# Projections of x in pairs by seven products over half of K, values loaded for two heads, keys doubled on GpSimd

## The chip, the cores and the metric

The kernel is one program on one core of a Trainium2 chip. The core has TensorE (PE; its weight loads are listed apart as PEld), VectorE (DVE), ScalarE (ACT), GpSimd (POOL) and SyncE (SP), which issues nearly all DMAs. The metric is the device time of one execution in microseconds. Before the change it is 2416.11 us, the median of three runs (2416.07 to 2419.38).

## The reference

The model is an encoder of two layers over 1024 tokens of width 1024, in float32. In each layer x is normalised and projected once; the columns of the projection belong to four groups of attention heads, which run side by side; their outputs are normalised, joined and projected back, and an MLP with squared ReLU follows.

```python
h = rms_norm(x, norm1_g[l])
proj = h @ w_in[l]
(a_cq, a_ckv, a_kr, b_q, b_k, b_v, c_q, c_k, c_v, d_q, d_k, d_v) = jnp.split(proj, splits, axis=-1)
y_a = mla_mixer(a_cq, a_ckv, a_kr, ...)      # A: latent attention, dense, 4 heads
y_b = diff_mixer(b_q, b_k, b_v, ...)         # B: difference of two softmaxes, dense, 4 heads
y_c = swa_mixer(c_q, c_k, c_v, sinks[l], ...)  # C: window of 128, 4 query and 2 key heads
y_d = na_mixer(d_q, d_k, d_v, na_rpb[l])     # D: neighbourhoods on a 2-D grid, 4 heads
mix = jnp.concatenate([rms_norm(y_a, ...), y_b, rms_norm(y_c, ...), rms_norm(y_d, ...)], axis=-1)
x = x + mix @ w_out[l]
h = rms_norm(x, norm2_g[l])
x = x + jnp.square(jax.nn.relu(h @ w_up[l])) @ w_down[l]
```

In front of A's attention stands a second projection: `a_cq` and `a_ckv` (the latents) are normalised by their own rows and multiplied by small matrices.

## The kernel before

**Numbers.** x lies transposed on the chip, as eight tiles of 128 features by 1024 tokens. Float32 matmuls go in three passes (`passes`): a weight is split into a high part `wh` and a low part `wl`, an operand into `xh` and `xl`, and wh·xh, wh·xl and wl·xh are added up in a bank of PSUM. A split (`split`) is one ACT instruction that writes the high part and one subtraction that writes the low one, on DVE for x and on GpSimd for the weights of the projections.

**Projections.** The columns of `w_in` are laid out as 15 tiles of 128 (`T_BQ`, `T_DK` and so on; A's are `T_CQ`, `T_CQR`, `T_CKV`) and the values of B and D apart in `w_v`. Three tiles go in an opening wave while x is being split (`several`), the values in `values`, and the other twelve by `one`: per tile the weights are loaded and split, and for each half of 512 tokens eight tiles of K in three passes make 24 matmuls of 128x512 in one bank. Then `ev` evicts the bank on DVE: times the row norms `rb`, for B and C with the rotary tables `tabc` and `tabs`, and the result is split again (tile `both`) and stored to HBM, from where the attention loads it in its own layout. `proj_latent` does A's tiles; it sums the squares of the latents (tiles `lsq`) by small matmuls on PE, makes the reciprocal roots on ACT and DVE, stores them as rows in HBM (`drows`) and loads them spread. `latent_up` then multiplies the latents (`latp`) by the second matrices.

**Attention.** Scores are matmuls of tiles `stack` (queries and keys with their high and low parts on top of each other, so that for D and C the key's 64 rows stand twice in a tile of 128), softmax is on DVE and ACT (tile `p`), PE transposes the probabilities (`ident,p`) and multiplies them by the values (`pt,v`). A's scores end in matmuls on tiles `corner`. `mix` are the attention's outputs as operands of the output projection, which is followed by the MLP (`far`, `opa`, `opb`, `opc`). The MLP is already built of seven products on halves of the tokens, of K and of the columns.

**Order.** No loop sets the order on the engines. Every instruction is first recorded (`Plan.add`), with what it reads and writes; `Plan.order` then walks through a model of the five queues and takes, on each engine, the ready instruction of lowest rank. Ranks come from a table `SPAN` by stage ('open', 'b1', 'lat', 'pd', 'pc', 'up', 'b', 'd', ...), limits on buffers from `ROOM` and `CAPS`. So projections, attention and the latents' second step are interleaved on PE, and each engine gets one fixed list. All are emitted from one line, L717, so the profile's rows are told apart by the names of tiles.

Of the kernel before, what the change touches and what calls it, by code (L numbers as in the profile page):

```python
# [23 lines left out]
P = 128  # L24
# [248 lines left out]
class Plan:  # L273
# [106 lines left out]
    def price(self, s):  # L380
# [3 lines left out]
        if op == "dma_start":  # L384
# [19 lines left out]
            per = (run / 20.7 if run >= 512 else 19.6 + run / 28.3) * (1.3 if few else 1.0)  # L404
# [190 lines left out]
    def issue(self, s, t):  # L595
# [13 lines left out]
        if q == "tensor":  # L609
# [13 lines left out]
            s.done = t + max(occ * (2 if s.tiled else 1), 220) + 180 * (1.5 if slow else 1)  # L623
# [10 lines left out]
class Place:  # L634


    def __init__(self, plan, bufs=1):
# [5 lines left out]
    ROOM = {'a4.0': 36, 'a4.1': 31, 'act10.0': 63, 'act10.1': 56, 'b4.0': 6, 'b4.1': 7, 'bias3.0': 4,  # L643
# [33 lines left out]
class Trunk:  # L677
# [106 lines left out]
    def product(self, ps, ws, xs, n, start=True, stop=True):  # L784

        last = len(ws) - 1
        for k, (w, x) in enumerate(zip(ws, xs)):
            self.passes(ps, w, x, slice(n * 512, n * 512 + 512), start and k == 0, stop and k == last)
# [1401 lines left out]
```

## Time and profile before

The profiled execution took 2422.19 us in all, its span is 2420.4 us; the three timed runs have a median of 2416.11 us.

| | busy us | share of the span | instructions |
|---|---|---|---|
| PE | 2387.2 | 99% | 12060 |
| DVE | 1861.2 | 77% | 3490 |
| ACT | 1300.1 | 54% | 2406 |
| POOL | 378.1 | 16% | 273 |

The mean granted clock of PE is 0.997, and 387.21 MB are moved by DMA, 160 GB/s on the average. A row of a group of instructions reads: line, engine, operation, what it writes and reads, shapes, how many; then busy us, mean ns of one; then the engine's idle time just before them and what ended it. The matmul's mean is from its start to a modelled end and overlaps the next one; the pace is the time of a stretch over its matmuls. A plain float32 matmul (`pt,v`, and the small ones on columns of ones) stands twice in the trace's counts.

### The profile page before, as it was taken

The numbers are of one execution on the slowest core, as the hardware profiler recorded it, in microseconds if no ns is written. First come the engines' busy times: TensorE is split into PE (matmuls) and PEld (weight loads), VectorE is DVE, ScalarE is ACT, GpSimd is POOL, SyncE is SP. The second block draws the span as 40 slices with busy tenths as digits, with TensorE's granted clock in tenths as the row PEclk, the third lists the DMA queues.
The fourth block names the chain that finished last, engine by engine and source line by source line (L and its number), as shares of the span: only waits on it lengthen the run. The fifth ranks groups of instructions, "written<-read, shape, count | busy, mean of one in ns | idle before, by whom it ended". The sixth has DMA issues, their size and how long they took to land.

```text
span 2420.4 us, 34855 instructions
## 1 busy us (share of the span) xinstructions
PE 2387.2 (99%) x12060; PEld 1904.4 (79%) x12060; DVE 1861.2 (77%) x3490; ACT 1300.1 (54%) x2406; POOL 378.1 (16%) x273
## 2 busy tenths in 40 slices
PE   9999999999999999999999999999999999999998
PEld 7877766778788888888887777767788888888887
DVE  6687776777977779778858778767598777898778
ACT  5555676664644445344435667676564444544446
POOL 4253025023000000000033231430410000000000
PEclk9999999999999999999999999999999999999999
DMA  6444798731444466443454376894514444755442
GB/s 204 135 139 136 190 256 240 181 123 55 140 147 158 160 219 203 151 150 109 153 166 113 114 188 178 240 253 125 170 46 161 152 147 158 243 166 166 137 136 92
DMA packets 213953, 387.21 MB, mean 160 GB/s; under 512 B 41720, under 2 KB 60304, under 8 KB 213776
## 3 DMA queue, kind: packets, MB, share of 16 engines
q1 hardware_dynamic: 198800, 358.76, 49.5%
q10 hardware_dynamic: 14976, 26.22, 2.9%
q8 instruction: 95, 1.56, 0.3%
q14 instruction: 82, 0.67, 0.1%
HBM read 268.80 MB, written 116.09 MB: 159 GB/s over the span
## 4 chain that ended last, share of the span: by engine, by line
PE 73%; DVE 6%; DMA 3%; ACT 2%; issue 1%; POOL 1%; SPq 0%; DVEq 0%; POOLq 0%; ACTq 0%
PE bank L717 73%; DVE p L717 1%; DVE x L717 1%; DVE part L717 1%; DMA ws<-in_w_out 1%; DMA rz<-drows 1%; DVE ev L717 1%; SPq L717 0%; DMA tabc<-in_c 0%; ACT p L717 0%; DVE far L717 0%; DMA drows<-row 0%; DVE xl L717 0%; DVE wl L717 0%; DVE sq L717 0%
## 5 line engine op out<-in xcount | busy, mean ns | idle before, releaser
L717 PE MATMUL bank<-far,wh 128*128 128x512 f32 (+1 forms) x2848 | 869.0, 387 | 0.0
L717 PEld LDWEIGHTS bank<-far,wh 128*128 128x128 f32 x2848 | 532.1, 188 | 109.5 <-ACT wh L717 0.9
L717 PE MATMUL bank<-far,wl 128*128 128x512 f32 (+1 forms) x1424 | 550.1, 387 | 1.8 <-DVE wl L717 1.7
L717 ACT ACTIVATE p<-p,col 128x1024 f32<-128x1024 f32 (+2 forms) x320 | 294.0, 920 | 97.4 <-DVE col L717 93.2
L717 POOL TENSOR_TENSOR wl<-ws,wh 128x512 fp32r<-128x512 f32 (+1 forms) x122 | 162.7, 1340 | 1016.3 <-DVE x L717 598.7
L717 PEld LDWEIGHTS bank<-far,wl 128*128 128x128 f32 x1424 | 267.5, 188 | 57.9 <-DVE wl L717 3.6
L717 DVE TENSOR_TENSOR x<-bank,x 128x512 f32<-128x512 f32 (+1 forms) x276 | 187.4, 682 | 125.7 <-PE bank L717 125.1
L717 PE MATMUL bank<-stack 96*128 96x512 f32 (+3 forms) x768 | 237.7, 391 | 2.0 <-DMA va<-part 0.9
L717 PE MATMUL bank<-ident,p 128*128 128x128 f32 x1376 | 219.6, 275 | 5.2 <-DVE p L717 4.5
L717 PEld LDWEIGHTS bank<-ident,p 128*128 128x128 f32 x1376 | 164.5, 140 | 44.2 <-issue 10.3
L717 PE MATMUL bank<-xh,wh 128*128 128x512 f32 x480 | 189.3, 405 | 1.6 <-ACT xh L717 1.5
L717 PE MATMUL bank<-xl,wh 128*128 128x512 f32 x480 | 190.2, 407 | 0.4 <-DVE xl L717 0.4
L717 DVE CUSTOM_DVE_ANT_0 p<-bank,zero 128x512 f32<-128x512 f32 x192 | 129.4, 686 | 79.0 <-PE bank L717 77.2
L717 PE MATMUL bank<-xh,wl 128*128 128x512 f32 x480 | 189.6, 406 | 0.4 <-POOL wl L717 0.4
L717 ACT ACTIVATE pt<-bank 128x512 f32<-128x512 f32 (+2 forms) x256 | 137.3, 558 | 92.9 <-PE bank L717 80.3
L717 ACT ACTIVATE far<-act 128x512 fp32r<-128x512 f32 x224 | 134.6, 622 | 86.8 <-DMA act<-acts 83.8
L717 DVE TENSOR_TENSOR wl<-raw,wh 128x512 fp32r<-128x512 f32 x224 | 153.6, 690 | 27.2 <-ACT wh L717 26.6
L717 PE MATMUL bank<-pt,v 128*64 128x256 f32 (+2 forms) x1344 | 164.4, 389 | 1.3 <-ACT pt L717 0.8
L717 PE MATMUL bank<-mix,wh 128*128 128x512 f32 x512 | 160.8, 394 | 3.5 <-ACT mix L717 2.6
L717 PEld LDWEIGHTS bank<-stack 128*128 128x128 f32 (+1 forms) x768 | 135.4, 189 | 35.2 <-issue 9.0
L717 ACT ACTIVATE ev<-ev 128x512 f32<-128x512 f32 x128 | 80.8, 632 | 139.5 <-DVE ev L717 136.5
L717 DVE CUSTOM_DVE_ANT_0 p<-bank,zero,col 128x512 f32<-128x512 f32 x192 | 142.4, 747 | 14.1 <-PE bank L717 5.6
(188 smaller groups left out, 3958.6 us busy)
## 6 DMA issues: line engine op xcount, KB each, us to landing
act<-acts SPq DMA_DIRECT2D x224, 256.0 KB
raw<-in_w_up SPq DMA_DIRECT2D x128, 256.0 KB
acts<-ev SPq DMA_DIRECT2D x128, 256.0 KB
acts<-ev ACTq DMA_DIRECT2D x96, 256.0 KB
c<-in_w_down SPq DMA_DIRECT2D x64, 256.0 KB
ws<-in_w_in SPq DMA_DIRECT2D x60, 256.0 KB
rz<-drows SPq DMA_DIRECT2D x40, 256.0 KB
ws<-in_w_out SPq DMA_DIRECT2D x40, 256.0 KB
```

The lines of the kernel that those rows point to most:

```text
L717: getattr(s.eng.engine, s.op)(*[real(a) for a in s.args], **{k: real(a) for k, a in s.kw.items()})
```

## The change

Each of the twelve tiles now goes together with another one: (BQ1, BK1), (CQ, CKV), (DK1, CQR), the two of DQ, the two of C's queries, (CK, CV). Of the eight tiles of K, two of the first four and their partners four further (`DEEP` = 2: tiles 0, 1 and 4, 5) are treated as a 2 x 2 block product: the two halves of tokens, the two halves of K and the two tiles of columns make seven products of blocks in place of eight. The other four tiles of K are multiplied as before. The products share banks of PSUM: a bank is read in between (by ACT into a tile `sum`, or by a DVE sum), and more products are accumulated into it.

For that, `sums` makes, once a layer, four combined operands for each of two tiles of x and their partners (tiles `tx`), overwriting the two tiles of x in place, and `two` makes combined weights from the loaded tiles `wr` on GpSimd, in pieces of two tiles of K (256 columns). The evictions read `sum` for part of the tiles. x's parts are now kept by halves of tokens. The stages b1, lat, pd, pc become 'vals', 'sums' and 'px', in which the latents come second, ahead of D's and C's tiles.

The loads of values take two heads at once (`vpair`: runs of 128 numbers in HBM, where they were 64), in B and D. The keys of D and C are loaded once into the first 64 partitions of their tile, and `again` copies them to the other 64 on GpSimd. `SPAN`, `ROOM` and two of the planner's costs (of DMAs, and of the end of a matmul) have new numbers.

```diff
-        def one(t, xs, ev):
-            ws = self.wtile(w_in(t))
-            for n in range(2):
-                ps = self.mm_ps()
-                self.product(ps, ws, xs, n)
-                ev(n, ps)
-                yield True
+        def two(ts, evs):
+            raw = []
+            for t in ts:
+                for c, w in enumerate(self.twin("wr", bufs=3)):
+                    raw.append(w.rearrange("p (k c) -> p k c", k=4))
+                    self.load(raw[-1], w_in(t)[c])
+            a, b, c, e = raw
+            J = self.DEEP
+            near = lambda t: t[:, :J]
+            add = partial(self.tt, eng=nc.gpsimd)
+            plain = [[xs[k + h][n] for h in (0, 4) for k in range(J, 4)] for n in range(2)]
+            def parts(*srcs):
+                wh, wl = (self.wp.tile([P, 4, P], R, tag="wd" + p, bufs=4, name="w" + p) for p in "hl")
...
+                    self.split(wh[:, sl], wl[:, sl], t, eng=nc.gpsimd)
...
+            def copy(ps):
+                t = self.place.tile([P, 512], F, tag="sum", bufs=3, name="sum")
+                nc.scalar.activation(t, ps, AF.Copy)
+                return t
+            def join(t, ps):
+                self.tt(t, ps, t, ALU.add)
+            u, q, r = self.bank("u"), self.bank("q"), self.bank("q")
+            wa = parts(a)
+            self.block(u, wa[:J], ops[1])
+            c11 = copy(u)
+            wb = parts(b)
+            self.block(q, wb[:J], ops[2])
+            self.block(q, wa[J:] + wb[J:], plain[0], False)
+            join(c11, q)
+            evs[0](0, c11)
+            self.block(r, wa[J:] + wb[J:], plain[1])
+            s1 = near(self.half_weights())
+            add(s1, near(c), near(e), ALU.add)
+            add(near(c), near(a), near(c), ALU.subtract)
+            add(near(a), s1, near(a), ALU.subtract)
+            add(near(b), near(b), near(a), ALU.subtract)
+            yield True
+            p = self.bank("p")
+            w5 = parts(s1, c[:, J:])
+            self.block(p, w5[:J], ops[5])
+            c12 = copy(p)
+            w6 = parts(near(a), near(c))
+            self.block(u, w6[:J], ops[6], False)
+            join(c12, u)
+            self.block(r, parts(near(b)), ops[3], False)
+            join(c12, r)
+            evs[0](1, c12)
+            yield True
+            self.block(u, w6[J:], ops[7], False)
+            c22 = copy(u)
+            we = parts(e)
+            self.block(p, w5[J:] + we[J:], plain[1], False)
+            join(c22, p)
+            evs[1](1, c22)
+            self.block(u, we[:J], ops[4], False)
+            self.block(u, w5[J:] + we[J:], plain[0], False)
+            evs[1](0, u)
+            yield True
+        def sums():
...
+            ops.update({1: [xs[k][0] for k in J], 2: [xs[k + 4][0] for k in J],
+                        3: [xs[k + 4][1] for k in J], 4: [], 5: [], 6: [], 7: []})
+            def parts(i, src):
+                t = self.place.tile([P, 2, 512], R, tag="tx", bufs=8, name="tx")
+                ops[i].append(self.rows_split((t[:, 0], t[:, 1]), src))
+            for k in J:
...
+                self.tt(t, v, t, ALU.subtract)
+                nc.scalar.activation(t, t, AF.Copy, scale=gk)
+                parts(5, t)
+                less(t, hi, t)
+                parts(6, t)
+                nc.scalar.activation(v, v, AF.Copy, scale=gk)
+                less(v, hi, v)
+                parts(7, v)
+                less(t, lo, t)
+                parts(4, t)
...
-        with at("b1"):
-            run_all(one(T_BQ[1], xs, self.ev_rope(tabs, qb[:, 1])))
-            run_all(one(T_BK[1], xs, self.ev_rope(tabs, kb[:, 1])))
+        with at("vals"):
             values(r)
+        with at("sums"):
+            sums()
...
+        with at("px"):
+            run_all(two((T_BQ[1], T_BK[1]), [self.ev_rope(tabs, qb[:, 1]), self.ev_rope(tabs, kb[:, 1])]))
+            run_all(self.proj_latent(l, two, d_keys(1), rb, tabs, lat, krd, rows))
             run_all(proj_d())
-        with at("pc"):
             run_all(proj_c())
...
-    BANKS = {"mm": 8, "tr": 4, "sb": 2, "pv": 2}
-    EARLY, NP = 4, 6
+    BANKS = {"mm": 8, "tr": 4, "sb": 2, "pv": 2, "u": 1, "p": 1, "q": 2}
+    EARLY, NP, DEEP = 4, 6, 2
...
+    def vpair(self, src, t):
+        v = self.place.tile([P, 8, P], F, tag="vv", bufs=2, name="vv")
+        self.load(v, src[:, :, t * P:t * P + P].rearrange("t p d -> p t d"))
+        return [v[:, :, j * 64:j * 64 + 64] for j in range(2)]
+    def again(self, k):
+        self.nc.gpsimd.tensor_copy(k[64:128], k[0:64])
...
-                    self.load(k[0].bitcast(F)[half], kd[0, t, rows])
-                for i in range(2):
-                    self.load(k[1].bitcast(F)[i * 64:i * 64 + 64], kd[1, t, rows])
+                    self.load(k[i].bitcast(F)[0:64], kd[i, t, rows])
+                for s in k:
+                    self.again(s)
```

The order of the instructions shows this at two places. Over the whole list PE has 11270 matmuls and transposes before and 11198 now.

The first place is on PE in layer 0, where the sums of the latents' squares are made (`lsq`; `stack` are scores, 384 columns wide for D and C and 512 for B, `ident,p` transposes, `x` and `wh` a projection). Before:

```order
L717 MATMUL bank_102<-pt,v 64x256 x16
L717 MATMUL bank_106<-stack 128x256 x2
L717 MATMUL bank_105<-stack 128x256 x2
L717 MATMUL bank_101<-lsq,square 32x256 x4
L717 MATMUL bank_101<-lsq,pairs 16x256 x4
L717 MATMUL bank_101<-lsq,more 32x256 x4
L717 MATMUL bank_103<-stack 128x384 x2
L717 MATMUL bank_100<-stack 128x384 x2
L717 MATMUL bank_107<-ident,p 128x128 x3
L717 MATMUL bank_104<-ident,p 128x128
L717 MATMUL bank_106<-ident,p 128x128
L717 MATMUL bank_104<-ident,p 128x128
```

Now:

```order
L717 MATMUL bank_107<-ident,p 128x128 x2
L717 MATMUL bank_100<-pt,vv 64x256 x16
L717 MATMUL bank_106<-lsq,square 32x256 x4
L717 MATMUL bank_106<-lsq,pairs 16x256 x4
L717 MATMUL bank_106<-lsq,more 32x256 x4
L717 MATMUL bank_101<-ident,col_72 8x128
L717 MATMUL bank_105<-stack 128x512
L717 MATMUL bank_102<-stack 128x512
L717 MATMUL bank_104<-stack 128x512
L717 MATMUL bank_103<-x_249,wh 128x512 x2
L717 MATMUL bank_107<-stack 128x512
L717 MATMUL bank_100<-x_354,wh 128x512
```

Before, all projections lie ahead of these rows, scores of D or C stand around them, and the first `latp` stands 118 rows later. Now a pair of D's tiles begins behind them, scores of B stand around them, and the first `latp` stands 455 rows later. Ahead of the first corner of A then lie, counted from the first `latp`, 109 transposes of probabilities in layer 0 (before: 66) and 112 in layer 1 (before: 128).

The second place is on POOL, at the end of layer 0's projections: `wl<-wr,wh` are low parts of weights, `part<-part` and `both<-part,both` C's rotary sums and low parts, `y<-y,rz` an output times its denominators. Before, no copies stand there. Now:

```order
L717 TENSOR_TENSOR wl<-wr,wh 128x256 x3
L717 TENSOR_TENSOR wl<-wr,wh 128x512
L717 COPY stack<-stack 64x1024 x2
L717 TENSOR_TENSOR part<-part 128x4x8x8 x2
L717 TENSOR_TENSOR both<-part,both 128x512 x2
L717 COPY stack<-stack 64x1024 x6
L717 TENSOR_TENSOR wl<-ws,wh 128x512
L717 COPY stack<-stack 64x1024 x4
L717 TENSOR_TENSOR y<-y,rz 128x1024
```

The twelve copies of a layer come behind the last low parts of the projections' weights; two of them stand ahead of the last rotary sums of C, and A's first low part (`wl<-ws,wh`) stands behind eight. On SP the loads `stack<-kd` and `stack<-kc` of a layer fall from 24 to 12 and those of B's and D's values from 8 to 4.

More of the change, by code (lines that the diff above doesn't have):

```diff
@@ L991, in d_keys @@
+        ops = {}
         def d_keys(t):
@@ L994, in proj_d @@
         def proj_d():
-            for t in range(2):
-                yield from one(T_DQ[t], xs, self.ev_plain(rb, self.to_parts(qd[:, t], 0.125)))
-            yield from one(T_DK[1], xs, d_keys(1))
+            yield from two(T_DQ, [self.ev_plain(rb, self.to_parts(qd[:, t], 0.125)) for t in range(2)])
         def values(r):
@@ L1199, in ev @@
             c, s = tabs
-            if rows and n == 0:
+            done = len(ys)
+            if rows and not ys:
                 ys.extend([self.part(), self.part()])
@@ L1288, in ev @@
             self.latent_parts(y, self.gq[:, l, 1:2], 64, n, lat[:, 1], squares[1])
-        yield from one(T_CQR, xs, ev)
+        yield from two((T_DK[1], T_CQR), [keys, ev])
         with self.plan.sooner(15):
@@ L1717, in attn_c @@
             for n, k in enumerate(ks[kv]):
-                for i in range(2):
-                    self.load(k.bitcast(F)[i * 64:i * 64 + 64], run(kc[n, kv]))
+                self.load(k.bitcast(F)[0:64], run(kc[n, kv]))
+                self.again(k)
         for g in range(2):
```

80 lines of the change are left out of this document (46 added, 34 removed), and 58 rows, old and new, of tables (ROOM, SPAN).

## The prediction

> **What bounds the kernel now.** I read the first part of the page first: who is busy.
>
> ```profile
> span 2420.4 us, 34855 instructions
> PE 2387.2 (99%) x12060; PEld 1904.4 (79%) x12060; DVE 1861.2 (77%) x3490; ACT 1300.1 (54%) x2406; POOL 378.1 (16%) x273
> ```
>
> TensorE (PE) is busy for 2387.2 of 2420.4 us; all else has room on the average. An average over stages can deceive, so next comes the busy time by stretch (columns: the stretch, its length, then busy time and instructions of PE, PEld, DVE, ACT and POOL, the granted clock, the DMA share and GB/s). Layer 0 has its projections with B's attention beside them at 30 to 310 us, the rest of the attention to 425, the end of A and the output projection to 612; 644 to 1193 is MLP alone; layer 1 follows from 1212.
>
> ```profile
> 30.00:310.00 280.00, 278.78 (x1464) 219.21 (x1462) 210.31 (x473) 158.69 (x284) 89.17 (x68) 1.00 0.53 147
> 310.00:425.00 115.00, 104.61 (x675) 73.74 (x675) 74.59 (x201) 81.88 (x217) 50.27 (x32) 0.97 0.97 250
> 425.00:612.00 187.00, 187.00 (x1123) 144.53 (x1120) 139.88 (x267) 114.45 (x202) 36.74 (x27) 1.00 0.40 114
> 644.00:1193.00 549.00, 548.95 (x2418) 453.43 (x2419) 435.14 (x698) 238.28 (x416) 1.30 (x1) 1.00 0.48 158
> 1212.00:1530.00 318.00, 314.38 (x1656) 246.10 (x1656) 232.29 (x511) 177.28 (x327) 95.87 (x70) 1.00 0.58 158
> 1530.00:1630.00 100.00, 96.16 (x660) 68.48 (x659) 74.37 (x199) 80.74 (x202) 39.15 (x26) 1.00 0.85 240
> ```
>
> In the projections PE idles 1.2 us of 280 in layer 0 and 3.6 of 318 in layer 1: there its work sets the time. In the stretch behind them it idles 10.4 us of 115 and 3.8 of 100; the DMA share is 0.97 and 0.85 there, and in layer 0 the granted clock falls to 0.97. So PE bounds nearly everything, and 14.2 us of waiting behind the projections are the one thing that a better order could still win.
>
> The chain of waits (start, length, what) shows both kinds of stretch.
>
> ```profile
> 343.35 11.90 DMA tabc<-in_c
> 355.32 7.12 DMA drows<-row
> 364.75 7.74 DMA stack<-qc
> 391.16 8.03 DMA rz<-drows
> 644.05 549.15 PE bank L717 x2418
> ```
>
> In the MLP it is one piece of PE: 549.15 us over 2418 matmuls, 0.2271 us each, the pace of a full-rate 128x512 matmul (the groups' mean of 387 to 407 ns overlaps the next matmul). Between 343 and 412 us it runs through DMAs instead, with PE filling in from other work.
>
> **The change part by part.** *PE work removed.* A pair of projection tiles took 2 tiles x 2 halves x 8 tiles of K x 3 passes = 96 matmuls. Now half of K goes by seven products of 2 x 3 = 6 matmuls, the other half stays at 4 x 12 = 48: 42 + 48 = 90. Six matmuls fewer, six pairs, two layers: 72. All are of the form of this row, of which there are three groups of 480:
>
> ```profile
> L717 PE MATMUL bank<-xh,wh 128*128 128x512 f32 x480 | 189.3, 405 | 1.6 <-ACT xh L717 1.5
> ```
>
> At 0.2271 us that is 72 x 0.2271 = **16.4 us**, taken out of a stretch in which PE has no idle time, so I count all of it.
>
> *Work added on the other engines.* The rows that price it, each of the nearest operation of the same shape:
>
> ```profile
> L717 DVE TENSOR_TENSOR ev<-bank,ev 128x512 f32<-128x512 f32 x96 | 66.2, 689 | 66.6 <-PE bank L717 40.9 <-ACT ev L717 25.5
> L717 DVE SCALAR_TENSOR_TENSOR t<-x,par,t 128x512 f32<-128x512 f32 x16 | 12.6, 812 | 0.0
> L717 DVE TENSOR_TENSOR far<-t,far 128x512 fp32r<-128x512 f32 x16 | 10.6, 693 | 0.9 <-ACT far L717 0.9
> L717 ACT ACTIVATE ev<-bank 128x512 f32<-128x512 f32 x96 | 57.3, 597 | 148.2 <-PE bank L717 147.6 <-ACT ev L717 0.4
> L717 ACT ACTIVATE wh<-ws 128x512 fp32r<-128x512 f32 x104 | 64.3, 623 | 47.9 <-DMA ws<-in_w_in 18.8 <-PE bank L717 13.1 <-DMA ws<-in_w_out 11.9
> L717 ACT ACTIVATE wh<-ws 128x256 fp32r<-128x256 f32 x18 | 7.4, 412 | 15.4 <-DMA ws<-in_w_out 10.6 <-PE bank L717 4.4 <-DMA ws<-in_w_lat 0.3
> L717 POOL TENSOR_TENSOR wl<-ws,wh 128x512 fp32r<-128x512 f32 x104 | 146.1, 1408 | 987.6 <-DVE x L717 598.7 <-ACT wh L717 245.4 <-DMA ws<-in_w_out 90.8
> L717 POOL TENSOR_TENSOR wl<-ws,wh 128x256 fp32r<-128x256 f32 x18 | 17.0, 948 | 28.7 <-PE bank L717 19.9 <-ACT wh L717 7.3 <-issue 1.5
> L717 POOL TENSOR_TENSOR y<-y,rz 128x1024 f32<-128x1024 f32 x16 | 39.0, 2442 | 50.3 <-DMA rz<-drows 48.1 <-ACT p L717 2.2
> L717 ACT ACTIVATE sq<-x 128x1024 f32<-128x1024 f32 x16 | 16.7, 1044 | 0.0
> ```
>
> Per layer: DVE gets 24 sums out of a bank (24 x 0.689 = 16.5 us), 6 scaled differences (6 x 0.812 = 4.9) and 10 low parts or differences of x (10 x 0.693 = 6.9): 28.3 us. ACT gets 18 copies out of a bank (10.7), 12 copies and scalings for the combined operands (12 x 0.623 = 7.5) and shorter high parts of weights, 30 of 256 columns for 6 of 512 (30 x 0.412 - 6 x 0.623 = 8.6): 26.8 us, and some 2 more for x split by halves. GpSimd gets the low parts, 30 x 0.948 - 6 x 1.408 = 20.0 us, 24 weight combinations of 256 columns at the same 0.948 or a little less (22.8), and 12 key copies of 64x1024. Such a copy does not stand in the trace: one input of 1024 columns takes ACT 1.04 us, two inputs take GpSimd 2.44; 12 of them cost 12.5 to 29.3 us. I take the upper end, since that row is GpSimd's own: 72 us in all.
>
> What hides it is the idle time of the same stretch in layer 0: DVE 280 - 210.3 = 69.7 us, ACT 121.3, GpSimd 190.8; in layer 1 it is more. So 28, 29 and 43 us (the copies come after the last weights) are costed at nothing. Were the cover gone, DVE's 28.3 us a layer would be the price, 56.6 in all.
>
> The reading that speaks against this is in the timeline (start, length, engine, instruction):
>
> ```profile
> 155.29 1.28 DVE L717 SCALAR_TENSOR_TENSOR p<-p,col 128x1024 f32<-128x1024 f32 x1
> ...
> 164.47 1.28 POOL L717 TENSOR_TENSOR wl<-ws,wh 128x512 fp32r<-128x512 f32 x1
> ...
> 164.99 1.83 DVE L717 SCALAR_TENSOR_TENSOR p<-p,col 128x1024 f32<-128x1024 f32 x1
> ```
>
> The same DVE instruction takes 1.28 us, and 1.83 when it begins while GpSimd is at a subtraction: 0.55 us more. The change adds to each layer 54 DVE instructions that read two operands from SBUF (38 evictions that now read the collected sum instead of a bank, 16 for the operands), while GpSimd's share grows from 89 to some 132 us of the stretch. All 54 lengthened would be 29.7 us: with the 28.3 that is 58, still under 69.7. The range of this term is 0 to 29.7 us of DVE a layer; half of it is my value, all of it hidden. The Trainium skill (SBUF — State Buffer, Who interferes with whom) has a rule for this: a DVE instruction with two SBUF inputs and a GpSimd instruction that reads SBUF exclude one another, and the later one blocks until the first is done. The trace agrees in kind, with 0.55 us of such a block; by that rule a collision could cost up to the whole GpSimd instruction, which the first rival below takes up.
>
> *New hand-overs.* The bank of a running sum is read and then accumulated into again four times a pair, three times behind ACT's copy (0.597 us) and once behind DVE's sum (0.689); PE must wait for the reader or have other work. Bounds: nothing, as in the MLP, which is built of the same seven products and idles 0.05 us in 549; or all of it, 36 x 0.597 + 12 x 0.689 = 29.8 us. The attention interleaved here is more and finer cover than the MLP has, so I take the end near nothing: 2 us.
>
> *DMA removed.* The keys of D and C lose 24 loads of 256 KB, 6.3 MB; B's and D's values go in 8 loads with runs of 512 B, not 16 with runs of 256 B.
>
> ```profile
> stack<-kd SPq DMA_DIRECT2D x32, 256.0 KB
> stack<-kc SPq DMA_DIRECT2D x16, 256.0 KB
> v<-vb SPq DMA_DIRECT2D x8, 256.0 KB
> ```
>
> At the 250 GB/s of 310 to 425 us the 3.1 MB of a layer are 12.6 us of transfer, just where the queues are full. What PE gets of that lies between nothing and its 10.4 and 3.8 us of idle time. The copies wait on GpSimd for their loads, and queued behind them are C's rotary sums and low parts, which only C's scores wait for, by then behind D's.
>
> *Work moved.* In the order shown above the latent norms stand on PE amid the projections, not behind them, so their round trip (rsqrt, store, spread load) passes under some 450 rows of work. In layer 0, 109 score transposes are then left between the first latent product and A's first corner, where 66 were; in layer 1 it is 112 for 128. So I let layer 0 give back 4 of its 10.4 us and layer 1 nothing.
>
> Sum: -16.4 + 2 - 4 = -18.4 us on the profiled span of 2420.4 us. The profiled run took 2422.19 us in all, the median of the runs is 2416.11, 6.1 less; the difference carries over: 2416.1 - 18.4 = **2398 us**.
>
> **Rivals.** *DVE becomes the bound* (slower). One stretch has no room left, the end of the projections:
>
> ```profile
> 270.00:310.00 40.00, 39.95 (x223) 31.63 (x221) 37.19 (x97) 29.73 (x59) 7.04 (x6) 1.00 0.97 232
> ```
>
> DVE is at 93% there, and the last two pairs of a layer (C) evict in or near it. If a third of the 58 us falls where DVE is full, PE stands 19.3 us a layer: 38.7 - 16.4 = +22, 2438 us. It decides from 8.2 us a layer on. Against it: DVE's 69.7 us of slack, and attention rows moved from the projections into the later, emptier stretch (139.9 us busy of 187). The rule of the Trainium skill (SBUF — State Buffer, Who interferes with whom) would make a hit dearer than 0.55 us, and so speaks for this one.
>
> *PE's waits go* (faster still). The early norms and the lighter queues remove most of the 14.2 us and the clock dip (3% of 115 us, 3.4): 16.4 + 12 = 28, 2388 us. For it: the chain through DMAs at 343 to 412 us. Against: the other waits there are of rows, values and mix operands, which do not move.
>
> *The gain goes into waits* (no change). Behind the projections the chain is not PE's but DMA's; if A's loads land no sooner, the shorter projections only leave less filler, and 12 to 16 of the 16.4 us come back as idle time: 2412 to 2416. Against it: 3.1 MB a layer fewer in those queues.
>
> *The removed matmuls are not worth their time.* That 72 are gone is counted in the order. But the blocks are of 6 matmuls instead of 24; if each of the 11 blocks of a pair exposed one weight load (267.5 us over 1424, 0.188) it would be 12 x 11 x 0.188 = 24.8 us, and the time 2424.
>
> ```profile
> L717 PEld LDWEIGHTS bank<-far,wl 128*128 128x128 f32 x1424 | 267.5, 188 | 57.9 <-DVE wl L717 3.6
> ```
>
> The MLP's blocks of 12 expose none.
>
> **How the numbers follow.** Forecast 0.50, with its own range of 2391 to 2405; waits gone 0.22; gain lost in waits 0.14; DVE 0.10; weight loads 0.04. A measurement here tells about 0.2%, 4.8 us, from no change: faster is below 2411.3. That takes the forecast, the waits gone and half of the third rival: 0.79. Same is the rest of the third and some of the fifth, 0.09; slower is DVE and the other part, 0.12. The range of 8 in 10 reaches into both the faster rival and the lost gain: 2384 to 2414 us.
>
> **What would show it.** PE: 72 matmuls fewer, the projections' stretch shorter by some 8 us a layer, and its idle time there still under 5 us. MLP: 0.227 us a matmul, unchanged. Behind the projections: PE idle 6 us instead of 10.4 in layer 0, the DMA share below 0.97. DVE under 90% in the projections. Wrong would be: PE waiting for DVE sums or GpSimd low parts by more than 8 us a layer (first rival), or idle time behind the projections above 20 us (third).

## The result and the profile after

The changed kernel takes **2439.89 us** (median of four runs, 2438.19 to 2443.8); the kernel before, in the same comparison, 2417.74 us. The ratio is 1.0094, 95% interval 1.0076 to 1.0111: 22 us slower. I had forecast 2398.

The first lines of the page after:

```profile
span 2436.3 us, 34980 instructions
PE 2388.2 (98%) x11988; PEld 1892.7 (78%) x11988; DVE 1931.6 (79%) x3585; ACT 1347.9 (55%) x2529; POOL 493.1 (20%) x393
```

The 72 matmuls are gone (12060 to 11988), and PE is not busy for less: 2388.2 us after 2387.2. Its idle time, span less busy, went from 33.2 to 48.1 us. That is 14.9 of the 15.9 us between the two spans; the 16.4 us of the removed matmuls came back inside the busy time (the end of the part on the prediction says where). The spans differ by less than the medians' 22 us, since the profiled execution of the kernel before (2422.19 us) is slower than its median and that of the changed kernel (2438.19 us) is its fastest. By stretch (same columns as before; the MLP starts 11 us later, so its stretch is moved by 11):

```profile
30.00:310.00 280.00, 270.20 (x1377) 209.44 (x1376) 239.14 (x474) 169.44 (x311) 144.99 (x124) 0.98 0.48 138
310.00:425.00 115.00, 108.25 (x721) 77.51 (x720) 85.80 (x240) 91.37 (x243) 55.30 (x36) 1.00 0.89 252
425.00:612.00 187.00, 183.63 (x1091) 137.78 (x1090) 127.38 (x252) 107.39 (x185) 37.79 (x28) 1.00 0.42 116
655.00:1204.00 549.00, 548.77 (x2420) 453.11 (x2418) 438.15 (x704) 243.68 (x423) 0.75 (x1) 1.00 0.48 159
1212.00:1530.00 318.00, 312.37 (x1613) 243.51 (x1613) 267.07 (x539) 197.80 (x370) 151.98 (x129) 0.99 0.52 151
1530.00:1630.00 100.00, 95.47 (x638) 68.52 (x635) 72.50 (x199) 77.43 (x204) 47.91 (x31) 1.00 0.87 247
```

In layer 0's projections PE idles 9.8 us where it idled 1.2, and the clock is at 0.98; 3.4 us more come in at 425 to 612, where it had idled nothing. Only the stretch behind layer 0's projections got better (6.8 for 10.4); in layer 1 both stretches idle a little more (5.6 for 3.6 and 4.5 for 3.8). The MLP is unchanged, 0.2268 us a matmul.

The list of what PE waits for (total us, times, longest us), before:

```profile
PE bank L717 <- DVE p L717: 4.5, 4, 1.6
PE bank L717 <- POOL wl L717: 1.9, 2, 1.4
PE bank L717 <- ACT p L717: 1.3, 3, 0.9
PE bank L717 <- ACT wh L717: 1.0, 1, 1.0
```

and after:

```profile
PE bank L717 <- DVE p L717: 8.7, 7, 4.3
PE bank L717 <- ACT p L717: 7.9, 16, 1.8
PE bank L717 <- ACT wh L717: 5.7, 6, 1.9
...
PE bank L717 <- POOL wl L717: 0.4, 1, 0.4
```

PE waits for the softmax rows `p` (16.6 us where it was 5.8) and for high parts of weights. It does not wait for the collected sums, nor for GpSimd's low parts. The longest wait, in the timeline (start, length, engine, instruction, in brackets the idle time before it):

```profile
193.74 0.48 PE L717 MATMUL bank<-x,wh 128*128 128x512 f32 x1
194.05 0.39 PE L717 MATMUL bank<-x,wl 128*128 128x512 f32 x1
194.07 1.40 DVE L717 TENSOR_TENSOR part<-sum,tabs 16x512 f32<-16x512 f32 x2
...
195.59 0.66 DVE L717 TENSOR_TENSOR part<-bank,rb 64x512 f32<-64x512 f32 x1
...
196.46 0.69 DVE L717 TENSOR_TENSOR part<-bank,tabc 48x512 f32<-48x512 f32 x1
197.19 1.82 DVE L717 SCALAR_TENSOR_TENSOR p<-p,col 128x1024 f32<-128x1024 f32 x1
...
199.07 1.33 PE L717 MATMUL bank<-ident,p 128*128 128x128 f32 x5 [4.30 <-DVE p L717]
```

In PE's list the projection's matmuls are over at 194.4 and, after three more transposes (to 194.8), those of the next row come, while in DVE's list four instructions of a projection's evictions (the tiles `part`, 2.75 us) stand ahead of the one that finishes that row. Over this stretch no engine is full (DVE 85%); the two lists don't fit each other.

### The profile page after: what moved, and what is told of

It is laid out like the page before. It is cut to its first block, busy times and chain, and to the rows that moved or that the text cites. A ratio compares the mean times of both kernels' runs of the same rounds, so it can differ in the third digit from the quotient of the medians.

```text
span 2436.3 us, 34980 instructions
## 1 busy us (share of the span) xinstructions
PE 2388.2 (98%) x11988; PEld 1892.7 (78%) x11988; DVE 1931.6 (79%) x3585; ACT 1347.9 (55%) x2529; POOL 493.1 (20%) x393
## 4 chain that ended last, share of the span: by engine, by line
PE 80%; DVE 5%; ACT 3%; issue 1%; DMA 1%; SPq 1%; POOL 0%; DVEq 0%; ACTq 0%
PE bank L717 80%; ACT p L717 2%; DVE p L717 1%; DVE ev L717 1%; DVE part L717 1%; SPq L717 1%; DVE x L717 1%; DVE far L717 0%; ACT pt L717 0%; DVE wl L717 0%; DVE t L717 0%; DVE mix L717 0%; DMA wr<-in_w_in 0%; DVE col L717 0%; DVE raw L717 0%
## 5 line engine op out<-in xcount | busy, mean ns | idle before, releaser
L717 POOL TENSOR_TENSOR wl<-ws,wh 128x512 fp32r<-128x512 f32 (+1 forms) x86 | 105.2, 1229 | 949.1 <-PE bank L717 634.3
L717 PE MATMUL bank<-ident,p 128*128 128x128 f32 x1376 | 228.6, 279 | 19.4 <-DVE p L717 8.7
L717 PE MATMUL bank<-x,wh 128*128 128x512 f32 x720 | 242.0, 408 | 5.7 <-ACT wh L717 5.3
L717 PE MATMUL bank<-stack 96*128 96x512 f32 (+3 forms) x768 | 243.5, 399 | 2.9 <-DMA stack<-kb 1.6
L717 PEld LDWEIGHTS bank<-x,wh 128*128 128x128 f32 x720 | 135.3, 191 | 39.7 <-ACT wh L717 8.4
L717 ACT ACTIVATE wh<-raw 128x512 fp32r<-128x512 f32 x224 | 134.3, 624 | 34.3 <-ACT ev L717 20.8
L717 DVE TENSOR_TENSOR far<-act,far 128x512 fp32r<-128x512 f32 x224 | 148.8, 690 | 2.9 <-ACT far L717 2.9
```

The costliest lines, as they stand in the source:

```text
L717: getattr(s.eng.engine, s.op)(*[real(a) for a in s.args], **{k: real(a) for k, a in s.kw.items()})
```

## The experiments

The question was which of these the 42 us between forecast and result are: GpSimd's collisions and lateness (theory A, my first rival), DVE's added instructions (B), or the order in which the planner put the work (C). Ratios are against the kernel before, with 95% intervals.

**The side work made light, order kept.** Three kernels keep the change's order on every engine and make the products' side work light at the moment of emission:

```diff
             for s in steps:
+                if s.mark == "quiet" and s.eng.name == "gpsimd":     # first and third
+                    s.eng.engine.memset(real(s.kw["out"]).bitcast(F), 0.0)
+                    continue
+                if s.mark == "short":                                # second and third
+                    s.kw.update({k: s.kw[k][:, 0:16] for k in ("out", "in0", "in1")})
```

("quiet": GpSimd's combined weights and low parts in `two`; "short": `join` and the differences in `sums`. Two counts in the expectations are off: GpSimd's low parts are 96, 36 of 512 columns and 60 of 256, and DVE's differences are 16, not 32, so that the second kernel takes 28 us off DVE, 1931.6 to 1903.7, and not 58.)

> The changed kernel with its order of instructions kept as it is on every engine. All that GpSimd does for the pairs of projection tiles (the 48 combined weight blocks and 60 low parts of weights of both layers, 42 of them or so of 256 columns) becomes a fill with zeros, which reads nothing from SBUF; so the products come out wrong, but each instruction still stands in its place. Theory A (the first rival: DVE instructions with two SBUF operands are lengthened by GpSimd, and GpSimd's low parts come late): the sums read from SBUF fall from 0.84-0.95 us to the 0.69 of those read from a bank, PE's waits for DVE and ACT in the projections go, and the time falls from 2439.9 to 2420-2428 us. Theory B (it is DVE's own added instructions): under 5 us, 2435-2440. Theory C (the order of the instructions leaves PE without work at places, whatever the other engines take): 2436-2440.

> The changed kernel with its order kept on every engine. The 48 sums of a bank into a collected tile and the 32 differences of x that make the operands of the products work on 16 columns instead of 512 (so the products come out wrong); that takes some 48 x 0.62 + 32 x 0.9 = 58 us off DVE in all, 29 a layer, nearly what I counted as its added work. Theory B (DVE's added work makes the softmax rows late that PE's transposes wait for): PE's 8.7 us of waits for p of DVE go to under 3, half-speed spells of the clock with them, 2418-2428 us. Theory A: DVE is lighter too, but its lengthened instructions stay: 2428-2436. Theory C: 2436-2440.

> Both cuts together: GpSimd's work for the pairs reads no SBUF and DVE's sums and differences are of 16 columns, order kept (the products come out wrong). If DVE and GpSimd are the whole cause (A and B together), this is where my forecast should come back: 2398-2410 us. If the order or the hand-overs set the loss (C), it stays above 2430. What it leaves above 2400 belongs to neither engine.

Measured: 2440.2 (1.0090, 1.0072 to 1.0108), 2439.5 (1.0087, 1.0071 to 1.0103) and 2435.1 us (1.0071, 1.0055 to 1.0087). The load did go: with both light, DVE is busy for 1881.8 us in place of 1931.6 and GpSimd for 387.0 in place of 493.1. The groups of instructions (busy us, mean ns) of the first, where the rotary sums now take what they take from a bank (688):

```profile
L724 POOL MEMSET wl<- 128x256 f32 x60 | 17.8, 312 | 14.5 <-DVE both L726 11.0 <-PE bank L726 2.3 <-DVE part L726 1.3
L726 DVE TENSOR_TENSOR part<-sum,tabs 64x512 f32<-64x512 f32 x32 | 21.9, 686 | 0.7
```

and the same group in the change:

```profile
L717 DVE TENSOR_TENSOR part<-sum,tabs 64x512 f32<-64x512 f32 x32 | 25.9, 808 | 0.7
```

So collisions are real: 0.12 us in each of these. The Trainium skill (SBUF — State Buffer, Who interferes with whom) has the rule that a DVE instruction with two SBUF inputs contends with a GpSimd instruction that reads SBUF. The trace agrees, with 808 ns beside GpSimd's subtractions and 686 beside its fills. Taking these collisions away brought nothing in the total (2440.2 for 2439.9). Not all of them went: GpSimd's low parts of the evictions (`both`) still read SBUF, and other evictions from `sum` hardly got shorter (`part<-sum,tabc` 950 to 911 ns, `part<-sum,rb` 843 to 872). With both engines light, only 4.8 us come back, and PE waits as before (the profiled execution is the slowest of its four, 2439.6 us):

```profile
PE bank L728 <- ACT p L728: 7.8, 16, 1.8
PE bank L728 <- DVE p L728: 6.7, 3, 3.9
PE bank L728 <- ACT wh L728: 6.7, 6, 3.3
```

A and B, as explanations of this kernel's 22 us, fall. C stands, so far by elimination; the orders further down test it.

**The products undone, tables kept.**

```diff
-            a, b, c, e = raw
-            ...                       # seven products
+            for t, ev in zip(ts, evs):
+                ws = self.wtile(w_in(t))
+                for n in range(2):
+                    ps = self.mm_ps()
+                    self.product(ps, ws, xs, n)
+                    ev(n, ps)
-        with at("sums"):
-            sums()
```

> The changed kernel with the seven products undone: each pair of tiles is two plain tiles again (96 matmuls, weights split once, sums straight from the banks), and the combined operands of x are not made. Key copies, value loads for two heads, planner prices and the tables of numbers stay those of the change; the planner sets the order anew, so the order shifts where instructions are gone. Output as the reference. Theory A or B (the products' side work costs more than the 72 matmuls): 2418 us of before less a few for the keys and values, 2410-2420. Theory C (the tables, or the keys, values and prices, cost the time): 16.4 us are added to the changed kernel's time, 2445-2460.

Measured 2433.7 us (1.0063, 1.0047 to 1.0079): neither. With 72 matmuls more it is 6.2 us faster than the change, and still 15 slower than before. So the products do not carry the loss; most of it is in what is left: keys, values, prices, tables, x's parts by halves and the new order of the stages. The 6.2 us are not the products' price alone, since this kernel's order is another one too.

**The small parts alone, on the kernel before.** One kernel has only the two prices (the planner's rate of DMAs and end of a matmul), one only the key copies, one keys and values.

> The kernel before with nothing changed but the planner's two prices (a matmul's end and a DMA's bandwidth, as the change has them). Every engine gets the same instructions as before in another order: some 600 of 7600 rows of PE's order move. Theory C (the order decides, and a table of numbers fits only the plan for which it was found): the same work takes 5 to 25 us more, 2422-2445 us. Theory A or B (the engines' load decides, not the order): 2418 us of before, plus or minus 4.

> The kernel before with the key copies alone: D's and C's keys are loaded once and doubled by GpSimd (24 loads of 256 KB fewer, 24 copies of 64x1024 more, at 1.16 us each in the changed kernel); prices, tables, projections and value loads as before. The order shifts only a little (330 of 7600 rows on PE). Theory C: the part itself costs nothing, 2415-2422 us. Theory D (the copies are what is late: a scores matmul now waits for DMA and then GpSimd): 2425-2435 us.

> The kernel before with the key copies and the value loads for two heads (8 loads with runs of 512 B in place of 16 with runs of 256 B, in tiles of 1024 columns instead of 512, which take a place of the larger kind); prices, tables and projections as before. With the run of the keys alone this gives the value loads' part. Theory C: their own traffic saves a few us at most, but the tables no longer fit the places that they need, so 2425-2445 us. Theory A or B: 2412-2420.

Measured: prices alone 2440.9 us (1.0090, 1.0073 to 1.0108); keys 2420.2 (1.0003, 0.9992 to 1.0014); keys and values 2449.2 (1.0124, 1.0106 to 1.0143), above the 2425 to 2445 that I had expected of theory C. The first is the clearest of all runs. No instruction is added, removed or resized, only the order is another, and it costs 23 us, as much as the whole change. Its page shows the same work and more idle time (45.0 us for 33.2):

```profile
span 2437.3 us, 34737 instructions
PE 2392.3 (98%) x12060; PEld 1904.7 (78%) x12060; DVE 1858.0 (76%) x3490; ACT 1303.3 (53%) x2406; POOL 381.0 (16%) x273
```

The key copies cost and bring nothing that can be measured; theory D falls. The 29 us that the value loads add can't be read as the loads' own price, since a new order comes with them too.

**The 72 matmuls alone.** The kernel before, its order kept, without 72 of the matmuls wh·xl of the twelve tiles (one or two of the eight tiles of K in each half).

```diff
+                if s.mark == "out":
+                    continue
```

> The kernel before in its own order, with 72 matmuls of 128x512 left out of the 24 tiles of which the change makes pairs (of the 24 matmuls of one half of a tile one is gone, of the other half two; the products come out slightly wrong). It measures the first term of my sum alone, with no side work and no new order. If the stretch is bound by PE, 72 x 0.2271 = 16.4 us: 2399-2404. If PE only reaches the next wait for a row or an operand earlier (theory F: the rows of the attention set the pace, the matmuls are filler), 2410-2418, and the waits grow by what is gone.

Measured 2409.2 us (0.9965, 0.9951 to 0.9978): 9.1 us below the kernel before, between my two expectations. That is 0.13 us a matmul instead of 0.227, and the interval (5 to 12 us) leaves 16.4 out. Its profiled execution (2407.18 us, the fastest of four) does not show theory F's longer waits:

```profile
span 2405.4 us, 34707 instructions
PE 2371.8 (99%) x11988; PEld 1889.0 (79%) x11988; DVE 1856.8 (77%) x3490; ACT 1300.4 (54%) x2406; POOL 381.9 (16%) x273
```

PE idles 33.6 us as before (33.2) and is busy for 15.4 us less. A part of that is the clock: this execution has no spell at half speed before its last 10 us, that of the kernel before has two (6.8 us). The other three executions have a lower mean clock (0.996 for 0.999). So the matmuls alone are worth less than their pace, and that the rest of them is filler ahead of the next wait is not shown.

**Other orders for the same work.** The due times (`SPAN`) and limits (`ROOM`) were searched anew under the planner's own rules, for the change and for plain pairs, and the side work was made light once more, now in the order found for the change. The last one rounds the due times of plain pairs to 0.01 us.

The stage of the pairs, as an example (the change's own numbers, the second set, and below it plain pairs with its set and that rounded):

```diff
-        'px': ((85.19, 112.02, 136.96, 221.89, 238.30, 266.14), (1309.72, 1335.25, 1366.10, 1450.72, 1465.40, 1498.71)),}
+        'px': ((85.85349453055034, 116.5473090837175, 154.4080449069935, 155.1733308482677, 178.10365674885563, 258.0584567480881), (1241.3916533722077, 1310.7898085588117, 1384.3180760470577, 1409.6638441916102, 1416.6823502501695, 1533.2172278706719)),
...
-        'px': ((110.89261501249177, 159.8238257062764, 197.8648703750341, 213.2809823011344, 246.4346569044656, 272.6347564892862), (1216.500701949237, 1227.2643057877988, 1387.9405901285922, 1387.9405901285922, 1472.4256609222807, 1542.9491597383944)),
+        'px': ((110.89, 159.82, 197.86, 213.28, 246.43, 272.63), (1216.50, 1227.26, 1387.94, 1387.94, 1472.43, 1542.95)),
```

> The changed kernel with other numbers in the two tables that set the order (the due times SPAN and the limits of places ROOM), found by a search with the planner's own rules and prices; code, instructions and output as the change. Theory C (the change's loss is that of its order): 2405-2425 us, 15 to 35 below the change, with PE's waits in the projections back to a few us and fewer half-speed spells. Theory E (the loss lies in what the seven products need: copies, hand-overs and combined weights, whatever the order): within 6 us of the change's 2440.

> The kernel with plain pairs (the change without the seven products) with its two tables found by the same search, as long as for the run before this. If the 72 matmuls are worth their 16.4 us once the order fits, this kernel is some 16 us slower than the changed kernel in its new order; if the products only trade PE's time for waits, the two are within 5 us. Theory C also has this one faster than with the change's own tables (2433.7): 2410-2428.

> The changed kernel in its re-found order, order kept, with the side work of the products made light as before: GpSimd's combined weights and low parts for the pairs become fills that read nothing, DVE's 48 sums and 32 differences work on 16 columns (the products come out wrong). In this order the seven products are 6.6 us dearer than plain pairs. If that is DVE's and GpSimd's load (theory B, now in an order that fits), it goes: 2404-2414 us. If it is the row of dependent blocks (bank filled, copied, filled again) and the fewer ways to place them, nothing changes: 2417-2422.

> The kernel with plain pairs in its re-found order, with the due times rounded to 0.01 us, which moves no due time by more than 0.005 us; the planner then gives another order (some 250 of 7300 rows of PE stand elsewhere). Instructions and output are the same. If an order only has to be about right, the time stays within 4 us of 2414. If the planner's greedy rules turn any small difference into another order, good or bad by chance (theory C in its strong form), it loses a good part of what the search had found: 2422-2435.

| kernel | us | ratio (95%) |
|---|---|---|
| the change, order found anew | 2420.9 | 1.0009 (1.0000 to 1.0019) |
| plain pairs, order found anew | 2414.2 | 0.9987 (0.9978 to 0.9996) |
| the change, order found anew, side work light | 2405.8 | 0.9941 (0.9925 to 0.9958) |
| plain pairs, due times rounded | 2431.9 | 1.0047 (1.0032 to 1.0062) |

Four things follow. The change's own instructions in another order take 19.0 us less. The first lines of that page:

```profile
span 2419.5 us, 35002 instructions
PE 2380.0 (98%) x11988; PEld 1891.2 (78%) x11988; DVE 1932.5 (80%) x3585; ACT 1347.0 (56%) x2529; POOL 499.5 (21%) x393
```

It has as many matmuls as the change, PE idle for 39.5 us in place of 48.1, and 13.7 us at half speed ahead of the last 10 us in place of 23.9. In its second order plain pairs are still 6.6 us ahead of the products, with 27.3 us of idle time on PE. The side work, which hardly counted in the bad order (4.8 us), is worth 15.1 us in the fitting one. The reading that a load shows only where no worse wait covers it fits this, but is argued. And a shift of due times by no more than 0.005 us costs 17.7 us (14.5 by the ratios): being nearly the same table did not keep the order good. The stretch behind layer 1's projections shows where a part of that goes; plain pairs first:

```profile
1515.00:1630.00 115.00, 114.41 (x786) 83.20 (x788) 80.29 (x235) 88.36 (x231) 36.03 (x23) 1.00 0.80 203
```

and rounded, with PE idle for 10.9 us in place of 0.6 (5.7 of it for DMAs into `corner`) and the clock at 0.96:

```profile
1515.00:1630.00 115.00, 104.11 (x675) 73.21 (x674) 73.55 (x211) 79.46 (x215) 37.34 (x24) 0.96 0.79 202
```

For the change's instructions in their three versions the time grows with PE's idle time ahead of the transposes of softmax rows (last part of the row: total, then by cause). It is not the whole: rounding plain pairs hardly moved this row (7.1 to 8.9 us). The kernel before, for comparison:

```profile
L717 PE MATMUL bank<-ident,p 128*128 128x128 f32 x1376 | 219.6, 275 | 5.2 <-DVE p L717 4.5 <-ACT p L717 0.4 <-DVE part L717 0.2
```

The change:

```profile
L717 PE MATMUL bank<-ident,p 128*128 128x128 f32 x1376 | 228.6, 279 | 19.4 <-DVE p L717 8.7 <-ACT p L717 7.9 <-DVE col L717 1.6
```

The change in its second order, and that with light side work:

```profile
L719 PE MATMUL bank<-ident,p 128*128 128x128 f32 x1376 | 220.3, 279 | 12.8 <-DVE p L719 5.7 <-ACT p L719 5.6 <-DVE y L719 0.5
```

```profile
L730 PE MATMUL bank<-ident,p 128*128 128x128 f32 x1376 | 218.4, 278 | 7.5 <-ACT p L730 4.8 <-DVE p L730 1.5 <-DVE part L730 0.2
```

Lighter DVE and GpSimd work takes away most of the waits for DVE's rows (5.7 to 1.5) and leaves those for ACT's. That is less than half of the 15.1 us: by the pages PE's idle time falls by 6.6 us in all (39.5 to 32.9) and its busy time by 9.2 (2380.0 to 2370.8), with 3.4 us at half speed where there were 13.7.

**Which side work, and is the gap chance?** Two kernels take GpSimd's and DVE's part by itself in that order, two more have a third set of numbers.

> The changed kernel in its re-found order, order kept, with only GpSimd's work for the pairs made light (combined weights and low parts are fills that read nothing; the products come out wrong). With GpSimd's and DVE's both light this order fell from 2420.9 to 2405.8 us. If it is the collisions (DVE's instructions with two SBUF operands lengthened while GpSimd reads SBUF) and GpSimd's own lateness, most of the 15 us goes here: 2406-2411. If it is DVE's own added instructions, 2418-2421.

> The same order with only DVE's sums and differences made light (16 columns; the products come out wrong), GpSimd as in the change. If DVE's added instructions are the price: 2406-2411 us. If the collisions are, 2416-2421. If both runs give about half, each engine's load is a part of it.

> The changed kernel with a third set of numbers in its tables, from a longer search (some 700 of 7300 rows of PE stand elsewhere than in the second). A second sample of a well-fitting order. If the second order's 2420.9 us is what the change is worth with a fitting order, this is within 5 us of it: 2414-2424.

> Plain pairs with a third set of numbers, from a search as long as for the run before this (some 1000 of 7300 rows of PE moved against the second). If plain pairs are really the cheaper ones, this is again 4 to 10 us below the changed kernel of the run before, 2408-2418 us; if the 6.6 us were chance of two orders, the two kernels can stand the other way round.

Measured: GpSimd light 2411.8 us (0.9971, 0.9959 to 0.9982), DVE light 2411.9 (0.9972, 0.9961 to 0.9983): each gives 9 of the 15.1, so each engine's load is a part of it, and they overlap. A collision needs both, and a row that is late for two reasons may be cured by either; these runs don't part the collisions from GpSimd's own lateness. The third orders: the change 2415.6 (0.9988, 0.9978 to 0.9997), plain pairs 2413.0 (0.9977, 0.9968 to 0.9987). The gap has the same sign and is 2.6 us, less than the 4 to 10 that I had expected and within the intervals. In none of three pairs of orders (6.2, 6.6, 2.6) did the seven products save anything. The pages agree: in the second and third orders PE idles 12.2 and 9.8 us more with the products (39.5 for 27.3, 34.3 for 24.5), and 6.6 and 5.8 us of that lie in layer 0's projections. Whether the products cost something stays open, since one order can be worth more than these gaps. Plain pairs in this order are the best version measured with the full computation, ahead of both kernels, of the kernel before by 0.2%.

**Keys and values in a fitting order.** The kernel before with the new prices and tables found for it:

> The kernel before with the change's two planner prices (as in the run that took 2440.9 us) and tables found anew for it by the same kind of search, somewhat shorter than for plain pairs. Instructions as before. Theory C once more: the 23 us that the prices' new order cost come back, 2410-2422 us. Against plain pairs in a fitting order (2414.2 and 2413.0 us) it has 24 key loads of 256 KB more, 24 key copies fewer, and values in single heads: if these loads matter once the order fits, it is 4 to 10 us above them; if not, within 3.

Measured 2424.8 us (1.0024, 1.0015 to 1.0033). That is above my 2410 to 2422; of the 23 us that the prices' order had cost, 16 come back. It is 10.6 and 11.8 us above plain pairs, as if the loads mattered; but its search was shorter, and no wait for a DMA stands in PE's list. Its longest wait, in the opening (ACT `xh`, 5.8 us), has its like in plain pairs (ACT `x`, 5.5 and 6.0 us) and explains nothing. Whether keys and values bring anything stays open. So does how far the kernel before is from its own best order: its tables were not searched anew with its own prices.

## Why the prediction was wrong

The bill goes from the changed kernel to the kernel before in three steps, so that its sum closes by itself: a badly fitting order 19.0 us (2439.9 less 2420.9; 24.3 with the third order); seven products against plain pairs, each in its second order, +6.6 (2420.9 less 2414.2; 2.6 in the third); keys, values and what the fitting order of plain pairs has over the old one -4 (2414.2 against 2418.3). Together +21.6, where 22.2 were measured. Only the first step is much larger than what separates two searched orders of one kernel (5.3 and 1.2 us).

- *"-16.4 ... taken out of a stretch in which PE has no idle time, so I count all of it."* Failed in its size. Alone it was 9.1 us; the other way round, 15.1 - 6.6 = 8.5, which fits but compares two orders. Busy 99.6% of a stretch did not make each matmul in it worth its pace. Where the rest stays is open: PE's waits did not grow when the matmuls were left out (33.6 us for 33.2).
- *"28, 29 and 43 us are costed at nothing"*, hidden in idle time of the stretch. Failed for DVE and GpSimd: of the 153 us of work that was taken off the two (DVE 1932.5 to 1882.9, GpSimd 499.5 to 396.2), 15.1 come through in a fitting order. DVE stayed at 85% of 30 to 310 us, as I had expected (under 90%), but its idle time did not lie where PE waited: four instructions ahead of one row went with a wait of 4.3 us. ACT's added work was not taken off by itself; its share is not known.
- *"Work moved ... layer 0 give back 4"*. This is the step that failed most. I priced one move in the new order, by its good side, and took all else of the order as free. The order of 7300 rows on PE was a new draw, and 19 to 24 us of the time are that draw. The two right readings (PE idle 6.8 us behind layer 0's projections where I had said 6; DMA share 0.89, below 0.97) came with 8.6 us more idle time ahead of them and 3.4 behind.
- *New hand-overs, 2 us.* Held: the change's list of PE's waits has no wait for a `sum`; in the second order there are two, 1.8 us together.
- *DMA and key copies.* The copies take 1.16 us each, near the lower of my bounds of 1.04 and 2.44 (I had taken the upper), and with the key loads that they replace they change nothing that can be measured, 0.9992 to 1.0014.
- *The first rival, 2438 us,* has nearly the measured time and not its cause. It asked for DVE to be the bound; DVE and GpSimd made light in that order leave 2435. That the numbers agree is chance. Its two ingredients are real, and cost 15 us in the second order. *Exposed weight loads* (2424) are not seen: the MLP keeps its 0.227 us, and from start to start the matmuls on `tx` take 0.233 us in the median. *The gain goes into waits* asked for more idle time behind the projections, where layer 0 has less (6.8 us for 10.4).
- *The signs.* Neither sign that I had named for being wrong came: no wait for DVE's sums or GpSimd's low parts above 0.4 us, no 20 us of idle time behind the projections. The sign that failed is the idle time in the projections, 9.8 us in layer 0 where I had said under 5.
- The range, 2384 to 2414, had no term for the order at all. The run with nothing but new prices shows how large that term can be: +23 us, more than the range is wide on either side of 2398.

Where the 16.4 us inside PE's busy time went can be counted in the two traces, from one start on PE to the next, against the same usual step for each shape (0.227 us for 128x512). The changed kernel has 16.4 us less work, 15.8 more in gaps of over 0.4 us, 7.7 more in spells at half speed and 8.9 more in shorter gaps, most of which the page counts as busy. The clock stood at half speed for 23.9 us (five spells, without the last 10 us of the execution) in place of 6.8.

## What to carry to other kernels

Where a greedy planner sets the order, every edit is also a new draw of the order, and here a draw was worth some 20 us of 2400, more than the edit: run the same instructions in several orders before crediting or blaming a change, and compare the two versions after the same search. Work taken off a bottleneck engine that is busy for 99% was here worth 9 us where its pace promised 16: leave the instructions out in place and measure, before counting them in full. A load on an engine that is not the bound can cost where its instructions stand ahead of the row that the bottleneck wants next, so read whose queue that row is in, not the average idle time.

## What the runs showed that I had not expected

The clock falls to half speed on a fixed grid. Ahead of the last 10 us, the changed kernel's spells begin at 9.13, 196.86, 210.51, 1412.01 and 1722.62 us in the trace's clock records: 0, 55, 59, 411 and 502 times 3.4133 us from the first, and the spells of the other runs that have several lie on such grids too. What goes with a spell is how busy PE was in the grid step before. Two waits of 1.81 us for ACT's rows, in A's stage of layer 1 and of layer 0, with their steps to within 0.12 us (the granted clock is the third number from the end):

```profile
1719.20:1722.60 3.40, 1.59 (x18) 0.89 (x15) 3.29 (x10) 3.40 (x7) 0.44 (x1) 1.00 0.69 264
1722.60:1726.00 3.40, 3.40 (x18) 3.09 (x15) 2.37 (x6) 1.65 (x4) 0.85 (x1) 0.50 0.03 6
...
517.60:521.00 3.40, 1.83 (x17) 1.07 (x18) 3.26 (x11) 3.27 (x6) 1.28 (x1) 1.00 0.02 5
521.00:524.40 3.40, 3.40 (x29) 2.43 (x31) 1.58 (x4) 1.60 (x3) 1.10 (x1) 1.00 0.02 3
```

The first wait falls within one step, PE is busy for 1.59 of 3.40 us, and the next step runs at half speed. The second reaches over a border, PE is busy for 1.83 of 3.40 (1.95 of 3.41 in the exact step), and nothing happens. I counted such steps in the traces of all nineteen kernels, several of which share an order, without the first 10 and last 12 us, where the step itself ran at full speed. Half speed followed 20 of the 21 steps in which PE was busy for less than 43%, 19 of 26 between 43 and 49%, 2 of 53 between 49 and 66%, and none above. So a wait of 1.8 us can cost up to 1.7 us more, half of a step (an estimate from these figures).

The Trainium skill (TensorE: Matmul & The Clock Gate, Part 1: The HAM clock gate) has a free-running step of 3413 ns and says that it takes an idle one to fall back. The traces agree with the step; they differ on the second, since a step that was nearly half busy was enough.
